# The sample's output projection in seven block products, with w_out's differences made beside w_in's pairs

## The chip, the cores and the metric

The kernel runs on one core of a Trainium2 chip. A core has TensorE for matmuls (PE in the profile; PEld is its weight load), VectorE (DVE), ScalarE (ACT), GpSimd (POOL) and SyncE (SP), whose queue issues nearly all DMAs. Each engine takes its own instructions in its own order and waits on semaphores for the others. Matmuls write to PSUM, of which the kernel uses eight banks of 128 x 512 fp32; SBUF holds everything else on the core. The metric is the device time of one execution in microseconds, the median over runs.

## The reference

One encoder layer on a prompt of 256 rows and a sample of 1024 rows, width 1024, with the same weights:

```
z = rmsnorm(x, g_mix) @ w_in                      # 1024 -> 5120: q, k, v of two branches, and gates
o_a = windowed attention with a sink (8 heads);  o_b = dilated attention (12 heads in 3 groups, merged)
merged = gates_a * (o_a @ w_a) + gates_b * (o_b @ w_b)
x = x + merged @ w_out                            # the output projection, 1024 x 1024
h = rmsnorm(x, g_mlp)
y = rmsnorm(x + square(relu(h @ w_up)) @ w_down, g_final)      # width 4096 inside
```

All of it is fp32. The kernel keeps the accuracy with matmuls on the type fp32r by splitting: a value becomes a high part (ACT copies it to the type fp32r) and a low part (DVE subtracts the high part), and a product is three matmuls: low by high, high by low, high by high.

## The kernel before, in words

The rows are ten tiles of 128: tiles 0 to 7 are the sample, 8 and 9 the prompt. The stages follow each other: values and normed x; w_in's columns in pairs (nine pairs alone, then seven beside the dilated attention); the windowed attention beside the last gates; the gate products; the output projection; the up projection; the down projection.

w_in's pairs, the up and the down projection already use the scheme of seven products (Strassen and Winograd): the sample's rows and the weight are cut into 2 x 2 blocks, A11 to A22 and B11 to B22, and instead of eight block products there are seven, of sums and differences: S1 = A21 + A22, S2 = S1 - A11, S3 = A11 - A21, S4 = A12 - S2 on the left, and T1 = B12 - B11, T2 = B22 - T1, T3 = B22 - B12, T4 = B21 - T2 on the right. The prompt's rows go through as plain products. `six` (line 342) issues the matmuls of one block product on one bank; `mm3` (line 188) the plain form.

*w_in's pairs.* `pair` (line 1039) issues the products of two columns of 128. Between them it calls `tick` (line 1115) 18 times a pair: it issues stores that are two ticks old, and later moves the dilated attention. `right_pair` (line 369) loads the next pair's weights on SP, makes the differences on POOL and the splits on ACT and DVE.

*Slots.* Nearly all SBUF is 33 slots of 4 KB a partition (`slot`), ten more for weights (`wslot`) and eight narrow ones (`qslot`). A tile gets a slot when one is free; the first instruction that writes it, often a DMA on SP, waits for the slot's last reader.

*Order.* Within `manual_schedule` each engine's instructions stand in the order in which the program writes them. That held for everything except the first half of the output projection, whose order a planner chose.

*The gate products* (loop at line 1527) are 48 products of 12 or 6 matmuls; each result is multiplied by its gate and added into `mT` on DVE. The list `side` beside them holds the splits that come next. w_out's blocks are loaded by `fetch` and split by `prepare` here and later.

*The output projection* (line 1646 on): for each half hh of the 1024 output columns and each of the ten tiles, 24 matmuls of 128 x 512 into one "mm" bank, then DVE adds the bank to the row tile `x2[t]`. Two tiles ahead, `split_m` splits `mT`. In the second half each tile is finished at once: ACT squares the row and takes the root (`ss`, `sd`), DVE scales it to `xn[t]`, SP stores the row to `scr_x`, and one tile later PE turns `xn` (`turned`, eight transposes, two banks) and ACT copies the turned tile out (`turn_sample`, `turn_prompt`). `more` and `sums` interleave w_up's first pair and the sums S1 to S3 of the turned rows. The prompt's tile 8 is turned in this loop, tile 9 in the up projection.

*The start of the up projection* (`up`, line 1947, with j = 0): the products A11, A12, S2, S3, S1, A22, then the next pair's A11 and A12, then S4 and the prompt. Between them `next(hooks)` runs one step of `entering` (line 2014): S3's split; tile 9 turned and S1's split; A22's split; S4's sums and split (`combine_last`); the prompt's split. `steps_of(b, 2)` runs what is left of the pair's own splits: none before, since the projection did them all.

## Time and profile before

| | |
|---|---|
| median of 3 runs | 1670.73 us (1670.70 to 1670.93) |
| the profiled execution's own time | 1671.05 us |
| its span, first to last instruction | 1669.3 us |
| PE busy | 1658.3 us, 9217 matmuls |
| DVE, ACT, POOL busy | 954.1, 715.1, 484.8 us |
| granted clock, mean | 0.999 |
| matmuls of the output projection | 480, first at 766.0 us |

Matmuls are pipelined: the duration of one overlaps the next, so PE shows as busy nearly all the time, and its pace is read from the distance between starts. In the chain of waits and in a timeline a row gives the start, the length, the engine and line, and in brackets the idle time before it with what ended it. In a table of stretches each engine's busy time stands in the order PE, PEld, DVE, ACT, POOL, then the granted clock, the DMA engines' share and GB/s.

### The profile page before, as it was taken

What the parts mean: (1) busy time and instruction counts of PE and PEld (TensorE: products, weight loads), DVE (VectorE), ACT (ScalarE), POOL (GpSimd) and SP (SyncE); (2) the same over time, 40 slices, a digit from 0 to 9 for tenths busy, and PEclk for the clock granted to TensorE, in tenths of its full rate; (3) what the DMA queues carried; (4) which work ended last, traced back from release to release, by engine and by line L of the source; (5) the groups of instructions that cost most, each with busy time, mean ns of one, the idle gap of its engine ahead of it and who ended that gap; (6) DMA issues with size and microseconds to landing.
All of it is one profiled execution on the core that took longest, in us unless ns stands there. A gap on an engine that the chain in (4) does not pass through costs nothing.

```text
span 1669.3 us, 24690 instructions
## 1 busy us (share of the span) xinstructions
PE 1658.3 (99%) x9217; PEld 1410.3 (84%) x9217; DVE 954.1 (57%) x1535; ACT 715.1 (43%) x1473; POOL 484.8 (29%) x362
## 2 busy tenths in 40 slices
PE   9999999999999999999999999999999999999998
PEld 7898888888888888788888888888888888888886
DVE  6732233455654565677378455455456775867665
ACT  6232323345654565654176333333334333333435
POOL 1212222121112353000100555455554250514240
PEclk9999999999999999999999999999999999999999
DMA  7416562666667795965111443343356934733333
GB/s 257 150 53 127 135 126 78 169 185 200 187 192 220 196 236 162 254 203 202 46 81 59 161 161 125 117 161 130 113 191 235 359 115 136 253 102 108 120 121 126
DMA packets 226993, 265.11 MB, mean 159 GB/s; under 512 B 29663, under 2 KB 156511, under 8 KB 226873
## 3 DMA queue, kind: packets, MB, share of 16 engines
q1 hardware_dynamic: 219816, 245.35, 46.5%
q0 software_dynamic: 6720, 17.65, 5.3%
q8 instruction: 73, 1.20, 0.3%
q10 hardware_dynamic: 336, 0.53, 0.1%
q14 instruction: 48, 0.39, 0.1%
HBM read 177.75 MB, written 90.96 MB: 161 GB/s over the span
## 4 chain that ended last, share of the span: by engine, by line
PE 95%; DVE 2%; ACT 1%; DMA 1%; issue 0%; SPq 0%; ACTq 0%
PE dn L346 22%; PE x L346 20%; PE mm L192 13%; PE z L346 10%; PE v L820 6%; PE y L346 5%; PE mm L346 5%; PE sc L346 3%; PE pv L346 3%; PE pv L1210 2%; PE pt L1194 2%; PE sc L554 1%; PE pv L601 1%; PE pt L587 1%; PE tr L337 1%; DMA sg<-scr_g 1%
## 5 line engine op out<-in xcount | busy, mean ns | idle before, releaser
L346 PE MATMUL dn<-dhi,ulo 128*128 128x512 f32 x448 | 174.3, 389 | 0.0
L346 PE MATMUL dn<-dlo,uhi 128*128 128x512 f32 x448 | 174.3, 389 | 0.0
L346 PE MATMUL dn<-dhi,uhi 128*128 128x512 f32 x448 | 174.3, 389 | 0.0
L346 PE MATMUL x<-chi,wlo 128*128 128x512 f32 x424 | 166.5, 393 | 0.0
L346 PE MATMUL x<-clo,whi 128*128 128x512 f32 x424 | 165.6, 390 | 0.0
L346 PE MATMUL x<-chi,whi 128*128 128x512 f32 x424 | 165.0, 389 | 0.0
L313 DVE TENSOR_TENSOR wlo<-ta,whi 128x1024 fp32r<-128x1024 f32 x30 | 55.7, 1855 | 173.4 <-ACT whi L311 173.4
L392 POOL TENSOR_TENSOR tb<-raw 128x512 f32<-128x512 f32 x25 | 32.7, 1307 | 410.6 <-PE mm L192 159.2
L313 DVE TENSOR_TENSOR wlo<-raw,whi 128x1024 fp32r<-128x1024 f32 x60 | 89.7, 1496 | 103.7 <-ACT whi L311 101.0
L346 PEld LDWEIGHTS dn<-dlo,uhi 128*128 128x128 f32 x448 | 84.1, 188 | 17.5
L346 PEld LDWEIGHTS dn<-dhi,uhi 128*128 128x128 f32 x448 | 84.1, 188 | 17.4
L346 PEld LDWEIGHTS dn<-dhi,ulo 128*128 128x128 f32 x448 | 84.1, 188 | 17.3
L346 PEld LDWEIGHTS x<-chi,whi 128*128 128x128 f32 x424 | 79.6, 188 | 16.9
L346 PEld LDWEIGHTS x<-chi,wlo 128*128 128x128 f32 x424 | 79.8, 188 | 15.2
L346 PEld LDWEIGHTS x<-clo,whi 128*128 128x128 f32 x424 | 79.8, 188 | 14.6
L1755 POOL TENSOR_TENSOR t<-raw,t 128x1024 f32<-128x1024 f32 x16 | 45.7, 2870 | 148.6 <-DMA raw<-in_w_down_dram 148.5
L186 DVE TENSOR_TENSOR ulo<-uraw,uhi 128x1024 fp32r<-128x1024 f32 x56 | 86.1, 1558 | 4.5 <-ACT uhi L185 4.5
L1906 DVE TENSOR_TENSOR v<-v,dn 128x512 f32<-128x512 f32 x90 | 59.7, 683 | 40.5 <-PE dn L346 38.5
L2006 POOL TENSOR_TENSOR u<-u,u 128x640 f32<-128x640 f32 x16 | 25.1, 1570 | 179.0 <-ACT u L1924 179.0
L186 DVE TENSOR_TENSOR dlo<-raw,dhi 128x1024 fp32r<-128x1024 f32 x32 | 50.5, 1601 | 45.2 <-ACT dhi L185 44.2
L346 PE MATMUL dn<-dhi,up 128*128 128x512 f32 x224 | 73.5, 389 | 0.0
L346 PE MATMUL z<-chi,wlo 128*128 128x512 f32 x184 | 71.6, 389 | 0.0
(319 smaller groups left out, 4605.3 us busy)
## 6 DMA issues: line engine op xcount, KB each, us to landing
scr_u<-u SPq DMA_DIRECT2D x112, 320.0 KB, 2.6
uraw<-scr_u SPq DMA_DIRECT2D x56, 512.0 KB, 4.4
raw<-in_w_down_dram SPq DMA_DIRECT2D x36, 512.0 KB, 7.0
raw<-in_w_up_dram SPq DMA_DIRECT2D x32, 512.0 KB, 5.5
raw<-in_w_in_dram SPq DMA_DIRECT2D x25, 512.0 KB, 5.4
sg<-scr_g SPq DMA_DIRECT2D x32, 256.0 KB, 5.9
uraw<-scr_u SPq DMA_DIRECT2D x28, 256.0 KB, 4.4
qk<-scr_kb SPq DMA_DIRECT2D x48, 128.0 KB, 2.8
```

The source lines that it names most:

```text
L186: nc.vector.tensor_tensor(lo, src, hi.bitcast(F32), op=ALU.subtract)
L192: nc.tensor.matmul(ps, a, b, start=i == 0, stop=i == len(seq) - 1)
L313: nc.vector.tensor_tensor(lo, src, hi.bitcast(F32), op=ALU.subtract)
L337: nc.tensor.transpose(ps[:, P * i : P * (i + 1)], xn[t][:, P * k : P * (k + 1)], ident)
L346: nc.tensor.matmul(ps, a, b, start=first and i == 0, stop=last and i == len(seq) - 1, skip_group_check=True)
L392: (nc.vector if vector else nc.gpsimd).tensor_tensor(o, x, y, op=ALU.subtract)
L820: nc.tensor.matmul(ps[:, :n], a, b, start=k == 0 and j == 0, stop=k == KC - 1 and j == 2)
L1194: nc.tensor.transpose(ps[:, P * k : P * k + P], s[:, h, P * b : P * b + P], ident)
L1210: nc.tensor.matmul(pv[HALVES[h], P * i : P * i + P], src, pt[:, at + 2 * b + h, :], start=b == 0, stop=b == W // P - 1, skip_group_check=True)
L1755: nc.gpsimd.tensor_tensor(o, a, b, op=ALU.subtract)
L1906: nc.vector.tensor_tensor(v, v, ps, op=ALU.add)
L2006: nc.gpsimd.tensor_tensor(u[S1], u21, u22, op=ALU.add)
```

## The change

Four parts.

1. *Differences ahead of time.* `differences` runs beside w_in's nine first pairs, one step a tick. In 16 rounds it loads a 128-column piece of w_out's four blocks into one slot (`wx`), makes T1 to T4 of it on DVE (in the order T1 and T3, T2, T4), splits them and stores high and low parts in DRAM (`scr_w`).
2. *Seven products.* Class `Out` writes the sample's projection as the products A12 by B21, S1 by T1, S4 by B22, A11 by B11, S2 by T2, S3 by T3, A22 by T4, each for four row tiles of 12 matmuls. A product's bank is added to one quarter of the rows (`TO`) and, where the scheme asks for it, stays open for the next product. T1 to T4 come from DRAM (`given`), the four blocks of w_out are loaded and split (`load`, `right`).
3. *36 steps in written order.* Each step is one group of 12 matmuls. The prompt's two tiles are cut by blocks: steps 4, 5, 18, 19 and 32 to 35. The list `side` gives each step's splits, sums, scalings and loads. `norm` (square, root, store) of tiles 0 to 3 is in steps 20 to 23, of tiles 4 to 7 in 28 to 31, of 8 and 9 in 33 and 35; `scale` follows in the next steps, and sample tiles are turned at the start of steps 23 to 26 and 31 to 34.
4. *The start of the up projection.* Both prompt tiles are scaled (behind S1's split) and turned (tile 8 behind `combine_last`, ahead of the product S1; tile 9 ahead of A22) there, and half of w_up's first pair's splits are left for it. S3's sums are made whole after the last turned tile.

```diff
         specs.append((w_b3[:, :, P * c : P * c + 4 * P], (P, 2, 4 * P), wslot))
     for c in range(0, KC, 2):
         specs.append((w_a3[:, :, P * c : P * c + 2 * P], (P, 4, 2 * P), wslot))
-    for h in range(2):
-        for i in range(4):
-            specs.append((w_out3[:, 2 * i : 2 * i + 2, 512 * h : 512 * h + 512], (P, 2, 512), wslot))
-    specs[n_out + 2] = specs[n_out + 2][:2] + (slot,)
     taken, raws = [0], []
...
+    scr_w = [dram.tile([P, 4, 4, 512], F32, name=f"scr_w{i}") for i in range(2)]
     scr_h = [dram.tile([P, 2, 2, 512], F32, name=f"scr_h{i}") for i in range(2)]
...
+        def differences():
+            blocks = w_out[0].rearrange("(a k p) (b c) -> p k a b c", a=2, p=P, b=2)
+            for i in range(16):
+                k, cols = i // 4, slice(P * (i % 4), P * (i % 4) + P)
+                x = slot("wx", (P, 8, P))
+                for a in range(2):
+                    nc.sync.dma_start(x[:, 2 * a : 2 * a + 2], blocks[:, k, a, :, cols])
+                for _ in range(3):
+                    yield
+                nc.vector.tensor_tensor(x[:, 4:6], x[:, 1:4:2], x[:, 0:2], op=ALU.subtract)
+                yield
+                nc.vector.tensor_tensor(x[:, 6], x[:, 3], x[:, 4], op=ALU.subtract)
+                nc.vector.tensor_tensor(x[:, 7], x[:, 2], x[:, 6], op=ALU.subtract)
+                yield
+                hi = stage("z", (P, 4, P), F32R, 2)
+                nc.scalar.activation(hi, x[:, 4:], AF.Copy)
+                yield
+                nc.vector.tensor_tensor(x[:, 4:].bitcast(F32R), x[:, 4:], hi.bitcast(F32), op=ALU.subtract)
+                yield
+                nc.sync.dma_start(scr_w[0][:, :, k, cols], hi.bitcast(F32))
+                nc.sync.dma_start(scr_w[1][:, :, k, cols], x[:, 4:])
+                yield
+                yield
+        apart = differences()
         def tick():
             ticks[0] += 1
             flush()
+            next(apart, None)
             n = ticks[0] - 18 * MIXED
             if n > 0 and n % 3 == 1:
                 next(att_b, None)
                 if first:
+                    run(apart)
                     att_b = attention_b(stage)
...
+        ORDER = (A12, S1, S4, A11, S2, S3, A22)
+        TO = (C11, C22, C12, C11, C12, C22, C21)
+        FIRST, LAST = (0, 1, 3), (0, 2, 6)
...
+        def load(self, name, k, h):
+            b = self.raw[name] = [self.make("oraw", (P, 2, 512)) for _ in range(2)]
+            for i in range(2):
+                j = 4 * k + 2 * i
+                nc.sync.dma_start(b[i], w_out3[:, j : j + 2, 512 * h : 512 * h + 512])
+        def right(self, name, i, make=wslot):
+            hi, lo = make("whi", (P, 2, 512), F32R), make("wlo", (P, 2, 512), F32R)
+            split(hi, lo, self.raw[name][i])
+            self.rights.setdefault(name, []).extend((hi[:, k, :], lo[:, k, :]) for k in range(2))
+        def given(self, name, n):
+            out = self.rights[name] = []
+            for i in range(2):
+                parts = [wslot("wt", (P, 2, 512), F32R) for _ in range(2)]
+                for x, src in zip(parts, scr_w):
+                    nc.sync.dma_start(x.bitcast(F32), src[:, n, 2 * i : 2 * i + 2, :])
+                out += [tuple(x[:, k, :] for x in parts) for k in range(2)]
...
+        def left(self, n, i):
+            hi, lo = slot("mhi", (P, 2, 512), F32R), slot("mlo", (P, 2, 512), F32R)
+            split(hi, lo, self.source(n, i))
+            self.lefts.setdefault(n, []).append((hi, lo))
+        def sum1(self, i):
+            self.s1.append(slot("s1m", (P, 2, 512)))
+            nc.vector.tensor_tensor(self.s1[i], mT.t[1, i], mT.t[1, 2 + i], op=ALU.add)
+        def sum2(self, i):
+            nc.vector.tensor_tensor(self.s1[i], self.s1[i], mT.t[0, i], op=ALU.subtract)
+        def sum3(self, i):
+            nc.vector.tensor_tensor(mT.t[1, i], mT.t[0, i], mT.t[1, i], op=ALU.subtract)
+        def sum4(self, i):
+            nc.vector.tensor_tensor(mT.t[0, 2 + i], mT.t[0, 2 + i], self.s1[i], op=ALU.subtract)
+        def split_prompt(self, k):
+            his, lo = [qslot("mph", (P, NP), F32R) for _ in range(4)], slot("mpl", (P, 4, NP), F32R)
+            src = mT.t[2, k]
...
+            self.pm[k] = [(his[c], lo[:, c, :]) for c in range(4)]
+        def add(self, t, h, ps):
+            v = x2[t][:, 512 * h : 512 * h + 512]
+            nc.vector.tensor_tensor(v, v, ps, op=ALU.add)
+        def product(self, n, t, name):
+            if n in self.FIRST:
+                tags = ("pt", "pt", "sc", "sc") if n == 1 else ("mm", "mm", "mm", "pv")
+                self.banks[t] = bank(tags[t], "wo")
+            lefts = [tuple(x[:, k % 2, P * t : P * t + P] for x in self.lefts[n][k // 2]) for k in range(4)]
+            six(self.banks[t], self.rights[name], lefts, n in self.FIRST, n in self.LAST)
+            c = self.TO[n]
+            return t + 4 * (c // 2), c % 2, self.banks[t]
+        def prompt(self, t, k, name, ps, first=True, last=True):
+            cols = slice(P * (t - 8), P * (t - 7))
+            six(ps, self.rights[name], [(hi[:, cols], lo[:, cols]) for hi, lo in self.pm[k]], first, last)
...
@@ -1529,15 +1629,24 @@
             load_gate(i + 8)
             for f, t in side_loads.get(i, ()):
                 f(t)
-            if i in (3, 24, 26, 31, 34, 38, 42):
+            if i in (3, 24, 26):
                 fetch()
-            if i > 41:
-                load_x2(i - 42)
+            if i == 28:
+                att_pool.close()
+                late = pre.enter_context(tc.tile_pool(name="late", bufs=1))
+                out.make = lambda name, shape=(P, D), dt=F32: late.tile(list(shape), dt, name=name, tag="l4", bufs=6)
+                out.load("b21", 1, 0)
+            if i in (40, 41, 42, 43):
+                load_x2(i - 40)
             open_gate(i + 2)
             for f, t in side.get(i, ()):
                 f(t)
-            if i in (38, 40, 42, 46):
-                prepare()
+            if i in (37, 39):
+                out.right("b21", (i - 37) // 2)
+            if i in (40, 41):
+                out.left(0, i - 40)
+            if i in (42, 44):
+                out.sum1((i - 42) // 2)
...
-            if i > len(jobs) - 6:
-                next(early_m, None)
-        run(split_m(1, 0, second_m))
-        last.close()
-    att_pool.close()
-    for t in range(len(x2), NT):
-        load_x2(t)
-        for q in (slice(0, 3 * P), slice(3 * P, 4 * P)):
+        for q in (slice(0, 2 * P), slice(2 * P, 3 * P), slice(3 * P, 4 * P)):
             for i in range(2):
                 nc.vector.tensor_tensor(s1[i][:, :, q], a21[i][:, :, q], a22[i][:, :, q], op=ALU.add)
-                yield
                 nc.vector.tensor_tensor(s2[i][:, :, q], s1[i][:, :, q], a11[i][:, :, q], op=ALU.subtract)
-                yield
-            for i in range(2):
-                nc.vector.tensor_tensor(a21[i][:, :, q], a11[i][:, :, q], a21[i][:, :, q], op=ALU.subtract)
-                yield
+            yield
+        for i in range(2):
+            nc.vector.tensor_tensor(a21[i], a11[i], a21[i], op=ALU.subtract)
...
+    def norm(t):
+        xn[t] = slot("xn", (P, D))
+        ss = small.tile([P, 1], F32, name="ss")
+        nc.scalar.activation(xn[t], x2[t], AF.Square, accum_out=ss)
+        sds[t] = small.tile([P, 1], F32, name="sd")
+        nc.scalar.activation(sds[t], ss, AF.Sqrt, bias=eps, scale=1.0 / D)
+        nc.sync.dma_start(scr_x[t], x2[t])
+    def scale(t):
+        rs = small.tile([P, 1], F32, name="rs")
+        nc.vector.reciprocal(rs, sds.pop(t))
+        nc.vector.scalar_tensor_tensor(xn[t], x2[t], rs, gm, op0=ALU.mult, op1=ALU.mult)
+    def first_left(k, i):
+        act[(A11, A12)[k]][i] = slot("chi", (P, 2, 512), F32R), slot("clo", (P, 2, 512), F32R)
+        split(*act[(A11, A12)[k]][i], raws_h[0, k][i])
...
+    def two():
+        steps_of(b0, 2)
+    gm = None
+    out.given("t1", 0)
+    for t in range(8, NT):
+        load_x2(t)
+    for t in range(4, 8):
+        load_x2(t)
+    out.load("b22", 1, 1)
+    S = lambda f, *a: (f, a)
+    keep = lambda name, shape, dt: out.make(name, shape, dt)
+    side = [[S(out.split_prompt, 1), S(out.left, 1, 0)], [S(out.left, 1, 1)], [S(out.sum2, 0)], [S(out.sum2, 1)],
+            [S(out.sum4, 0)], [S(out.sum4, 1)],
+            [S(out.left, 2, 0)], [S(out.left, 2, 1), S(out.right, "b22", 0, keep)], [S(out.right, "b22", 1, keep)],
+            [S(out.load, "b11", 0, 0), S(out.left, 3, 0)],
+            [S(out.right, "b11", 0)], [S(out.right, "b11", 1), S(out.left, 3, 1)],
+            [S(out.given, "t2", 2), S(out.sum3, 0)], [S(out.sum3, 1)],
+            [S(out.split_prompt, 0)], [S(out.left, 4, 0)], [S(out.left, 4, 1)], [S(load_g), S(out.left, 5, 0)],
+            [S(out.left, 5, 1)], [S(out.given, "t3", 1)],
+            [S(out.left, 6, 0)], [S(scale, 0)], [S(scale, 1)], [S(out.given, "t4", 3), S(out.load, "b12", 0, 1), S(scale, 2)],
+            [S(next, b0), S(scale, 3)], [S(next, b0), S(out.left, 6, 1)], [S(two)],
+            [S(first_left, 0, 0), S(first_left, 0, 1)],
+            [S(out.right, "b12", 0)], [S(scale, 4), S(first_left, 1, 0)], [S(scale, 5), S(out.right, "b12", 1)],
+            [S(scale, 6)], [S(scale, 7), S(first_left, 1, 1)], [S(next, sums)], [S(next, sums), S(two)], []]
+    plan = [(0, t) for t in range(4)] + [(8, 1, "b21"), (9, 1, "b21")]
+    plan += [(n, t) for n in (1, 2, 3) for t in range(4)] + [(8, 0, "b11"), (9, 0, "b11")]
+    plan += [(n, t) for n in (4, 5, 6) for t in range(4)]
+    names = ("b21", "t1", "b22", "b11", "t2", "t3", "t4")
+    for step in range(36):
+        turning = iter(())
+        if 23 <= step < 27:
+            turning = turn_sample(step - 23)
+        elif 31 <= step < 35:
+            turning = turn_sample(step - 27)
+        next(turning, None)
+        done = None
+        if step >= 32:
+            t = 8 + (step - 32) // 2
+            if step % 2 == 0:
+                ps = bank("sc", "wo")
+                out.prompt(t, 1, "b22", ps, last=False)
...
-            for t in range(NT):
-                m = parts.pop(t)
-                ps = bank("mm")
-                run(mm3(ps, [(m[k], (ws[k // 2][0][:, k % 2, :], ws[k // 2][1][:, k % 2, :]))
-                             for k in range(KC)]))
-                if hh == 0:
-                    nc.vector.tensor_tensor(x2[t][:, sl], x2[t][:, sl], ps, op=ALU.add)
-                    part(t + 2)
-                    if 2 <= t < 6:
...
-                turning = (turn_sample if t < 9 else turn_prompt)(t - 1) if t else iter(())
-                next(turning, None)
-                nc.vector.tensor_tensor(x2[t][:, sl], x2[t][:, sl], ps, op=ALU.add)
-                xn[t] = slot("xn", (P, D))
...
-                nc.vector.scalar_tensor_tensor(xn[t], x2[t], rs, gm, op0=ALU.mult, op1=ALU.mult)
-                nc.sync.dma_start(scr_x[t], x2[t])
-                next(turning, None)
...
+                out.prompt(t, 0, "b12", ps, first=False)
...
+        else:
+            n, t = plan[step]
+            done = out.product(n, t, names[n])
+        next(turning, None)
+        if done:
+            out.add(*done)
+        if 20 <= step < 24 or 28 <= step < 32:
+            norm(step - 20 if step < 24 else step - 24)
+        elif step in (33, 35):
+            norm(8 + (step - 33) // 2)
+        for f, a in side[step]:
+            f(*a)
+    run(sums)
+    run(halves(S2, combined[S2]))
+    last.close()
+    pre.close()
+    ctx.enter_context(tc.manual_schedule(engines=ALL))
...
             run(halves(S3, combined[S3]))
             yield
+            run(halves(S1, combined[S1]))
+            scale(8)
+            scale(9)
+            yield
+            run(halves(A22, combined[A22]))
+            yield
+            combine_last()
+            run(turn_prompt(8, ("pt", "sc")))
+            yield
             run(turn_prompt(9, ("pt", "sc")))
-            run(halves(S1, combined[S1]))
-            yield
-            run(halves(A22, combined[A22]))
-            yield
-            combine_last()
-            yield
             yield
             split_prompt()
             yield
```

93 lines of the change are left out of this document (31 added, 62 removed).

## The prediction

> **What bounds the kernel now.** I read the page first: its span, the busy times and the chain of work that ended last.
>
> ```profile
> span 1669.3 us, 24690 instructions
> ...
> PE 1658.3 (99%) x9217; PEld 1410.3 (84%) x9217; DVE 954.1 (57%) x1535; ACT 715.1 (43%) x1473; POOL 484.8 (29%) x362
> ...
> PE 95%; DVE 2%; ACT 1%; DMA 1%; issue 0%; SPq 0%; ACTq 0%
> ```
>
> TensorE sets the time: 95% of the chain is PE. So a matmul removed is worth its pitch, and another engine's work costs nothing until PE has to wait for it. The second view is the chain in order of time around the output projection, then one line's instructions.
>
> ```profile
> 832.32 5.46 PE mm L192 x24
> 838.66 5.46 PE mm L192 x24
> ...
> 892.52 2.72 PE z L346 x12
> ...
> 897.96 2.72 PE z L346 x12
> ```
>
> ```profile
> L192 PE MATMUL mm<-whi,mlo x160: 389/389/476, 766.0 to 881.3; 128*128 128x512 f32 x160
> ```
>
> The duration of one matmul (389 ns) overlaps its neighbour's. The pitch is what counts: 5.46/24 = 2.72/12 = 0.227 us. The eight transposes that turn a tile fill the gap 838.66 - 832.32 - 5.46 = 0.88 us. The projection is 3 x 160 = 480 matmuls from 766.0 on: 480 x 0.227 = 108.8, with nine turned tiles 7.9 more, 116.7. The next PE work begins at 881.96 (row below), 116.0 after the start, so PE never stops there. The waits of PE from 700 to 900 us confirm it:
>
> ```profile
> PE mm L192 <- DVE mT L1551: 1.1, 1, 1.1
> PE y L346 <- ACT praw L1577: 0.2, 1, 0.2
> ```
>
> The third view is busy time by stretch of 10 us.
>
> ```profile
> 760.00:770.00 10.00, 10.00 (x68) 9.27 (x67) 8.33 (x19) 4.18 (x13) 0.00 (x0) 1.00 1.02 405
> ...
> 800.00:810.00 10.00, 10.00 (x46) 8.28 (x45) 2.29 (x7) 0.00 (x0) 5.07 (x4) 1.00 0.00 1
> ...
> 880.00:890.00 10.00, 9.83 (x52) 8.02 (x51) 9.90 (x16) 6.30 (x11) 0.00 (x0) 1.00 0.56 154
> 890.00:900.00 10.00, 10.00 (x46) 8.28 (x45) 9.96 (x10) 7.28 (x10) 0.00 (x0) 1.00 0.02 5
> ```
>
> The columns are PE, PE's weight loads, DVE, ACT, POOL. In the middle of the projection DVE is idle three quarters of the time. Where the up projection starts (880 to 900) DVE is full (9.90 and 9.96 of 10) and PE only just does not wait. That is the place to watch.
>
> **What the change removes.** 36 steps of 12 matmuls are 432, so 48 matmuls go: 48 x 0.227 = **10.9 us**. Turned tiles are ten in both kernels. The new path from the first matmul to the end of step 35 is 36 x 2.72 + 8 x 0.88 = 105.0 us where nothing waits. All splits, additions and sums then have to fit into steps of 2.72 us (3.60 with a turned tile) instead of tiles of 5.46 (6.34).
>
> **What a step's chain costs.** The order is as written on each engine. In a step with `norm` and a split, DVE adds, ACT squares and takes the root, ACT copies the high part, DVE makes the low part, and only then may DVE add the next step. The durations (DVE and ACT timelines):
>
> ```profile
> 826.04 0.69 DVE L1682 TENSOR_TENSOR x<-x,mm 128x512 f32<-128x512 f32 x1 [4.75 <-PE mm L192]
> 832.30 0.68 DVE L1682 TENSOR_TENSOR x<-x,mm 128x512 f32<-128x512 f32 x1
> 832.90 1.22 DVE L313 TENSOR_TENSOR wlo<-raw,whi 128x1024 fp32r<-128x1024 f32 x1
> 834.52 0.16 DVE L1692 RECIPROCAL rs<-sd 128x1 f32<-128x1 f32 x1 [0.41 <-ACT sd L1687]
> 834.72 1.28 DVE L1693 SCALAR_TENSOR_TENSOR xn<-x,rs,gm 128x1024 f32<-128x1024 f32 x1
> 835.92 1.44 DVE L186 TENSOR_TENSOR mlo<-mT,mhi 128x256 fp32r<-128x256 f32 x4
> ```
>
> ```profile
> 827.93 1.28 ACT L1687 ACT_TABLE_LOAD   x1
> 829.23 0.29 ACT L1687 ACTIVATE sd<-ss,eps 128x1 f32<-128x1 f32 x1
> ...
> 830.66 1.05 ACT L311 ACTIVATE whi<-raw 128x1024 fp32r<-128x1024 f32 x1
> ...
> 834.20 0.29 ACT L1687 ACTIVATE sd<-ss,eps 128x1 f32<-128x1 f32 x1
> ```
>
> An addition takes 0.69 (0.60 to the next DVE instruction), a high part 1.05, a low part 1.22, `scale` 0.16 + 1.28 (1.40 in a row). From an addition's start to the root: 3.48 at the first tile, because of the table load, then 834.49 - 832.30 = 2.19. I let DVE start 0.2 after the step's last matmul is issued.
>
> *Tile 0* is turned at the start of step 23; its `scale` is in step 21, behind step 20's split of `left(6,0)`. From the end of step 20: 0.2 + 3.48 = 3.7 root, 4.7 high part, 5.9 low part, 6.4 after the addition of step 21, 7.9 `scale`. PE is there after two steps, 5.44: it waits **2.5**. The table load alone is 1.28 of it.
>
> *Tile 4* is turned in step 31; `scale(4)` stands in step 29, behind step 28's `norm` and `right("b12", 0)`. Same chain with the short root: 0.2 + 2.19 + 1.05 + 1.22 + 0.6 + 1.45 = 6.7 against 5.44: 1.3. To this comes w_up. How long loads of 512 KB take, shortest, median and longest, by w_in's in the pairs:
>
> ```profile
> DMA to landing us min/median/max: 4.0/5.4/8.5
> ```
>
> w_up's first raw is the seventh 512 KB load that SP issues after step 23 (four of `t4`, two of `b12`): 7 x 0.524 MB at the 405 GB/s of the row for 760 us is 9.1, SP starts about 0.9 after the step because it stands behind the store of tile 3, and the landing adds about 2.7 (the shortest 4.0 less 1.3 of transfer). So it lands 12.7 after step 23. ACT wants it after three steps of 3.60, at 10.8. ACT's high parts of step 26 and 27 then end at 13.8, 14.7, 15.7 and DVE's last low part at 17.9; step 28's addition was due at 16.4. 1.5 later: tile 4 waits **2.7**, bounds 1.3 (load early) and 5 (load 2.5 later).
>
> *Tiles 5 and 6* follow steps that again hold addition, root, high and low part in series, 0.69 + 1.48 + 1.05 + 1.22 = 4.4 (1.48: the 2.19 less the addition and its handing over), against 3.60: **0.75** each. Together 6.7 in the middle.
>
> A rule of the Trainium skill bears here ("SBUF — State Buffer", section "SBUF: two separate sides"): a DVE instruction with two inputs in SBUF and a GpSimd instruction that reads SBUF exclude each other for a whole instruction. The trace agrees:
>
> ```profile
> 952.36 1.75 POOL L392 TENSOR_TENSOR ta<-raw,tb 128x512 f32<-128x512 f32 x1
> ...
> 952.88 2.31 DVE L313 TENSOR_TENSOR wlo<-raw,whi 128x1024 fp32r<-128x1024 f32 x1
> ```
>
> That low part takes 2.31 instead of 1.22, behind a difference that GpSimd had begun. GpSimd's four differences of w_up fall into steps 27 and 28 by the sum above; by the rule tile 4 would wait one to two such delays, 1.1 to 2.2, longer, and the end would be 1678.3 to 1679.4. I leave it out of the sum: there, where each step's chain waits for ACT, DVE has gaps that can take it.
>
> **The end, where DVE is full.** Step 35's addition is the last thing of the projection; all that follows stands behind it on DVE. The rows of before:
>
> ```profile
> 881.96 1.03 PE L337 MATMUL tr<-ident,xn 128*128 128x128 f32 x8
> ...
> 883.76 0.41 DVE L1604 TENSOR_TENSOR s<-hraw 128x256 f32<-128x256 f32 x1
> 884.21 0.43 DVE L1606 TENSOR_TENSOR s<-s,hraw 128x256 f32<-128x256 f32 x1
> ...
> 887.46 2.35 DVE L313 TENSOR_TENSOR clo<-s,chi 128x1024 fp32r<-128x1024 f32 x2
> ...
> 889.73 2.36 DVE L313 TENSOR_TENSOR clo<-hraw,chi 128x1024 fp32r<-128x1024 f32 x2
> ...
> 890.49 1.09 ACT L1577 ACTIVATE praw<-tr 128x512 f32<-128x512 f32 x2
> ...
> 892.00 0.68 DVE L1927 TENSOR_TENSOR u<-y,c 128x512 f32<-128x512 f32 x1
> ...
> 893.33 2.36 DVE L313 TENSOR_TENSOR clo<-s,chi 128x1024 fp32r<-128x1024 f32 x2
> ...
> 899.00 2.35 DVE L1617 TENSOR_TENSOR hraw<-hraw,s 128x1024 f32<-128x1024 f32 x2
> ```
>
> ```profile
> 900.32 2.20 ACT L185 ACTIVATE chi<-hraw 128x1024 fp32r<-128x1024 f32 x2 [3.03 <-DVE hraw L1617]
> ```
>
> A pair of low parts or sums is 889.73 - 887.46 = 2.27, one is 1.14; relu and square 893.33 - 892.00 = 1.33; four sums of a 256 quarter 1.6. From the end of step 35 on DVE: start 0.2, addition 0.6, last quarter 1.6, S3 sums 2.27, S2 2.27, `tb` 1.14, S3 2.27, relu 1.33, `raw[1]` 1.14, S1 2.27, `scale(8)` 1.4: **16.5**. PE reaches tile 8's transposes after A11, A12, S2, S3 = 10.9: it waits about 5.6 (a part of it already at S2 and S3). New in this list against before are `tb`, `raw[1]`, one more `scale`, and S3's sums whole instead of their last quarter (2.27 for 0.8): 5.2 us on an engine without room.
>
> Next: `scale(9)` 17.9, A22 20.2, the next pair's first low part 21.3, the S4 sums 23.7. ACT has S4's high parts ahead of tile 8's two copies: 24.7, then 25.8. PE turned tile 8 until 17.5 and did S1 until 20.2. Tile 9's second half needs an "sc" bank; one is held by `z`, the other by tile 8 until that copy. So PE waits until 25.8, and A22 starts at **26.3** (half a turn later). Before it started at 897.96 - 881.96 = 16.0 after the projection, with the same transposes and groups between. Cost 10.3. Upper bound: one port delay and one late load more, 13. Lower bound: without the bank wait, A22's low parts are still at 20.2, so A22 starts at about 20: 4.
>
> **Beside w_in's pairs.** 16 rounds of two loads, three small differences, a split and two stores. DVE's work is at most 3 x 0.42 for the differences (256 elements a row or fewer) and 0.69 for the low part, 2.0 a round, 31 us in nine pairs where DVE is under a third busy:
>
> ```profile
> 100.00:200.00 100.00, 100.00 (x539) 89.09 (x538) 29.21 (x27) 27.70 (x40) 21.64 (x21) 1.00 0.56 119
> ```
>
> w_in's own loads land after 5.4 (row above). A wait for a 256 KB load stands on DVE just behind the addition of `y` or `x`, and the next of these that PE needs comes over 2.7 later, so a load that lands at 5.4 is hidden; the long store row of the query pairs on SP may delay one or two. I take 0.5, bounds 0 and 4 (three rounds at 8.5 less 2.7 would be more, but not all meet a matmul). **Steps 0 to 19** need 1.9 to 3.3 a step on DVE (an addition and one to three low parts or sums), 2.0 on average, under 2.72. Their loads: `t1`, six x tiles and b22 are 12 x 0.524 MB, 15.5 at 405 GB/s, from the last gate products on; x is wanted from step 4 (13.6), b22 in step 7 (21.8). b11 waits for b22's splits of step 8, lands about when ACT wants it in step 10, and has until step 14. Nothing; if that cover is gone, the load's lateness counts.
>
> **Sum.** From the first matmul to A22: 105.0 + 6.7 + 26.3 = 138.0; before 897.96 - 766.0 = 132.0. +6.0, with the pairs +6.5. The profiled run took 1671.05 (span 1669.3); its median is 1670.73, 0.3 less. 1671.05 + 6.5 - 0.3 = **1677.2**. The 10.9 saved are more than given back as waits.
>
> **Rivals.**
>
> *The order does not bind, and it gets faster.* If `scale` and the copies of tiles 8 and 9 ran when ready (both roots are ready 3 us after step 35), PE would wait for none of the turned tiles in the middle, and at the end A22 would be late only by DVE's 5.2 more work. Then 105.0 + 21 = 126 against 132: 1670.7 - 6 + 0.5 = 1665. The point: `scale(8)` ends less than 10.9 after step 35. For it speaks that ACT has room there; against it that ACT's `chi` at 900.32 sat 3.03 idle for DVE with later work ready behind.
>
> *The clock falls in the long waits.* The granted clock in the last stretches:
>
> ```profile
> 1660.00:1665.00 5.00, 2.56 (x12) 1.78 (x10) 2.70 (x7) 3.08 (x8) 0.00 (x0) 1.00 0.54 210
> 1665.00:1670.00 5.00, 0.00 (x0) 0.00 (x0) 0.37 (x1) 0.40 (x1) 0.00 (x0) 0.53 0.27 105
> ```
>
> It falls to 0.53 a few us after the last matmul. PE would idle 4.5 and 5.6 us at tiles 8 and 9; if the 12 matmuls after each ran at 0.53, that is 2 x (2.72/0.53 - 2.72) = 4.8: 1682. The Trainium skill ("TensorE: Matmul & The Clock Gate", Part 1) says that the clock halves after an idle window of about 3.4 us; no wait before is that long, so this trace shows only the end.
>
> *The scratch path blocks the pairs.* SP waits for the slot of the differences until both stores land, and w_in's loads queue behind. If each of the nine pairs lost 0.7: 1683. Against: a round has nine of a pair's 18 ticks, over 10 us (seven groups of 2.72 and two of the prompt a pair), for two landings of 5.4.
>
> *The waits come to two thirds of the sum* (w_up early, low parts not needed at a group's first matmul): 11.3 instead of 17.0, 1670.7 - 10.9 + 11.3 + 0.5 = 1671.6.
>
> **Numbers.** Forecast 58%, free order 13%, clock 11%, pairs 6%, two thirds 12%. A change under 0.2% (3.3 us) cannot be told here. Slower: forecast, clock, pairs, less the forecast's own lower edge, 0.71; same 0.16; faster 0.13. The forecast's own range is 1672 to 1682 (middle 5 to 9, end 7 to 13); the range for all is 1668 to 1684.
>
> **What would show it.** Right: PE waits for `xn` at the transposes of tiles 0, 4, 5, 6 and 8 (2.5, 2.7, 0.75, 0.75, about 4.5) and for the prompt copy at tile 9 (about 5.5); 9169 PE matmuls; DVE full for 25 us behind step 35. Wrong: PE without waits from 766 to 910, or waits in the pairs between 119 and 345, or a granted clock under 1 near 890.

## The result, and the profile after

The changed kernel takes **1718.02 us** (median of 6 runs, 1714.69 to 1719.62) against 1670.83 beside it (1670.56 to 1671.13): 1.0279 times, 95% interval 1.0266 to 1.0293. That is 47.2 us slower. The forecast was 1677.2, its range ended at 1684: the sign was right, the size far off. The profiled execution took 1716.08 (span 1714.3), 45.0 more than the one of before; the places below are read from it.

The page of the changed kernel, the same lines as before:

```profile
span 1714.3 us, 24750 instructions
...
PE 1663.6 (97%) x9169; PEld 1410.0 (82%) x9169; DVE 992.7 (58%) x1565; ACT 715.8 (42%) x1431; POOL 496.0 (29%) x362
...
PE 84%; DMA 7%; DVE 4%; ACT 2%; issue 1%; SPq 1%; POOL 0%; DVEq 0%; ACTq 0%; POOLq 0%
```

The 48 matmuls are gone (9217 to 9169), yet PE is busy 5 us longer, and DMA's share of the chain has grown from 1% to 7%. Stretches of the span show where (PE, weight loads, DVE, ACT, POOL, then PE's granted clock):

```profile
100.00:200.00 100.00, 88.86 (x463) 78.52 (x462) 32.83 (x43) 26.74 (x40) 19.31 (x18) 0.95 0.63 145
...
860.00:865.00 5.00, 4.29 (x16) 3.67 (x17) 2.61 (x4) 3.27 (x10) 0.00 (x0) 0.66 0.51 210
...
935.00:940.00 5.00, 0.33 (x3) 0.09 (x1) 5.00 (x5) 2.97 (x4) 0.00 (x0) 0.97 0.00 0
```

Before, PE was busy for 100 of 100 in the first row, at clock 1.00. What PE waits for, first from 95 to 400, then from 700 to 960:

```profile
PE x L341 <- ACT c L1079: 10.8, 4, 3.5
PE x L341 <- DVE long L965: 10.2, 1, 10.2
```

```profile
PE tr L332 <- DVE xn L1739: 5.1, 2, 2.7
PE tr L332 <- ACT praw L1677: 4.8, 1, 4.8
PE tr L332 <- DVE rs L1738: 2.5, 1, 2.5
```

So there are two losses. In **w_in's pairs** PE waits 21.0 us. The first product of the projection starts at 795.57 (timeline), not at 766.0: 29.6 later, and the 8.6 that no wait explains are slow matmuls behind the waits. From **the projection's first product to A22's** it takes 941.28 - 795.57 = 145.7 instead of 132.0: 13.7 more. Together 43.3 of the 45.0; A22's own group, at a slow clock, is 1.0 more (3.68 for 2.72), and 0.7 has no place yet.

The pairs, by the chain of waits:

```profile
129.08 19.82 DMA scr_w<-wx
...
148.99 0.59 SPq L1118
...
149.63 2.64 DMA wx<-in_w_out_dram
...
152.46 0.43 DVE wx L1121
152.88 0.99 DVE long L965
...
153.91 4.94 PE x L341 x12
158.86 2.75 PE y L341 x12
```

A store of the differences (256 KB) takes 19.82. SP waits for it, because the next round's load goes into the same slot. Then DVE waits for that load (L1121), and behind it on DVE stands `long` (L965), the addition that PE waits for. PE then needs 4.94 for 12 matmuls, 2.2 more than its usual 2.72.

The up projection's start, by the same view:

```profile
909.19 5.47 PE wo L341 x24
...
917.98 2.27 DVE hraw L1708 x2
920.25 4.54 DVE clo L308 x4
...
935.72 2.28 DVE hraw L1715 x2
...
938.09 1.06 ACT chi L185
939.14 0.98 ACT praw L1677 x2
...
940.17 1.11 PE tr L332 x4
941.28 3.68 PE z L341 x12
```

Step 35 ends at 914.66, A22 starts at 941.28, 26.6 later. This is the prediction's chain: DVE's list, S4's sums and high part ahead of the prompt's copy, then tile 9's second half.

### The profile page after: what moved, and what is told of

It reads as the page before. It is cut to its first block, busy times and chain, and to the rows that moved or that the text cites. A ratio compares the mean times of both kernels' runs of the same rounds, so it can differ in the third digit from the quotient of the medians.

```text
span 1714.3 us, 24750 instructions
## 1 busy us (share of the span) xinstructions
PE 1663.6 (97%) x9169; PEld 1410.0 (82%) x9169; DVE 992.7 (58%) x1565; ACT 715.8 (42%) x1431; POOL 496.0 (29%) x362
## 4 chain that ended last, share of the span: by engine, by line
PE 84%; DMA 7%; DVE 4%; ACT 2%; issue 1%; SPq 1%; POOL 0%; DVEq 0%; ACTq 0%; POOLq 0%
PE dn L341 22%; PE x L341 16%; PE z L341 8%; PE mm L192 8%; PE v L816 6%; PE wo L341 4%; DMA scr_w<-wx 4%; PE y L341 4%; PE mm L341 3%; PE sc L341 3%; PE pv L341 3%; PE pt L1219 1%; PE pv L1235 1%; PE sc L550 1%; PE pv L597 1%
## 5 line engine op out<-in xcount | busy, mean ns | idle before, releaser
L387 POOL TENSOR_TENSOR tb<-raw 128x512 f32<-128x512 f32 x25 | 37.4, 1496 | 502.5 <-DMA raw<-in_w_up_dram 314.1
L341 PE MATMUL z<-clo,whi 128*128 128x512 f32 x184 | 72.2, 392 | 0.0
```

Source lines behind the costliest of these rows:

```text
L341: nc.tensor.matmul(ps, a, b, start=first and i == 0, stop=last and i == len(seq) - 1, skip_group_check=True)
L387: (nc.vector if vector else nc.gpsimd).tensor_tensor(o, x, y, op=ALU.subtract)
```

## Experiments

Each time is a median. The kernel before, run beside each of them, took 1670.7 to 1672.2.

**No rounds.** The rounds of differences are left out; the projection loads parts of h21 in their place.

```diff
-        apart = differences()
+        apart = iter(())
-                for x, src in zip(parts, scr_w):
-                    nc.sync.dma_start(x.bitcast(F32), src[:, n, 2 * i : 2 * i + 2, :])
+                for x, src in zip(parts, scr_h):
+                    nc.sync.dma_start(x.bitcast(F32), src[:, i])
```

> The differences are left out: no rounds beside w_in's pairs; the projection loads parts of h21 in the place of the four differences, so its output is not the reference's. Its work is the same. Theory 1 (the rounds cost what is lost between 119 and 360): TensorE does not wait in the pairs, 29.6 us come back, about 1688.5. Rival (the pairs lose by something else, such as another placing of code or data): 1710 to 1718. If 1688 comes, the rest, 17 to 18 us over before, is the projection and the start of the up projection alone.

Measured: 1687.98 (1.0104 [1.0089, 1.0119] times before). PE waits for nothing between 95 and 400; the first product of the projection starts at 765.43, and A22 911.74 - 765.43 = 146.3 later, as in the changed kernel (145.7). The rounds cost all of the 30 us; what is left, 17, belongs to the projection and the up projection's start.

**Own raw blocks.** The next load no longer waits for the stores of the round before.

```diff
-                x = slot("wx", (P, 8, P))
+                r = stage("z", (P, 4, P), F32, 2)
...
+                x = slot("wx", (P, 8, P))
...
-                hi = stage("z", (P, 4, P), F32R, 2)
+                hi = x[:, :4].bitcast(F32R)
```

> The raw blocks of a round go into the two z tiles, the high parts over the slot's own first half: the next round's loads on SP no longer wait for the stores of the round before; DVE's first difference does, five ticks later. Theory 1a (one slot: SP's load waits for slow stores, and everything behind it is late): at least two thirds of the 29.6 come back, 1690 to 1699. Rival 1b (the loads of 512-byte pieces are themselves late beside GpSimd's broadcasts, whatever they wait for): 1708 to 1718.

Measured: 1715.11. My first theory fell: PE still waits 21.0. The chain of waits of this run:

```profile
122.79 20.45 DMA z<-in_w_out_dram
...
143.36 0.44 DVE wx L1122
...
145.01 0.59 ACT c L1079
145.59 0.04 issue
145.64 5.49 PE x L341 x12
```

Now the load itself, 128 KB, takes 20.45. The tile `wide` of this run, from 90 to 365:

```profile
L295 POOL DMA_DIRECT2D wide<-scr_l x6: 700/704/907, 120.4 to 259.3; - x6
...
DMA to landing us min/median/max: 10.4/10.7/22.3
```

GpSimd issues its first broadcast (2 MB, the longest) at 120.4; with 22.3 it ends at 142.7, the load at 143.24.

**No stores.** The rounds compute, but store nothing.

```diff
-                nc.sync.dma_start(scr_w[0][:, :, k, cols], hi.bitcast(F32))
-                nc.sync.dma_start(scr_w[1][:, :, k, cols], x[:, 4:])
```

> The rounds make the differences and their parts but do not store them; the projection loads parts of h21 in their place, so its output is not the reference's. Theory 1a: the slot is free as soon as the low part is made, SP never waits for a store, and nearly all comes back: 1689 to 1693. Rival 1b: the loads still wait behind the broadcasts: 1705 to 1715.

Measured: 1697.41 (1690.62 to 1700.67), between the two theories: 20.6 of the 30 come back. Loads land after 4.0 in the median, 16.1 at most. Stores and loads are both late.

**Broadcasts elsewhere.** GpSimd's six broadcasts go into the stage of the values, whose rows are then stored from SP's queue.

```diff
+            if t == 5:
+                run(line(0))
...
+            if t in (5, 6, 7, 8, 9):
+                run(line(t - 4))
...
-                        hooks = line(j) if j < len(LINES) else iter(())
+                        hooks = iter(())
...
-            nc.gpsimd.dma_start(scr_v[rows, 512 * v : 512 * v + NV[v]], vo)
+            nc.sync.dma_start(scr_v[rows, 512 * v : 512 * v + NV[v]], vo)
```

> GpSimd's six broadcasts to wide stand in the stage of the values (one after the store of the lines, five in its second half), not beside the pairs; that stage's value rows are stored from SP's queue. The rounds of differences are unchanged. Theory 1c (a load or store of 512-byte pieces lands only with the end of a broadcast that runs beside it: 128 KB in 20.5 us for 122.8 to 143.2 in the run with the raw blocks apart): every landing in the pairs falls to some 3 us, TensorE waits nowhere in them, 1686 to 1692. Rival 1d (the rounds' place in the order on SP, DVE and ACT, without the broadcasts): above 1705.

Measured: 1712.07. The total says no, the trace says yes. The tile `scr_w` between 95 and 365, and PE's waits from 0 to 400:

```profile
DMA to landing us min/median/max: 2.6/2.8/5.4
```

```profile
PE v L816 <- ACT vo L824: 10.0, 1, 10.0
PE tr L332 <- DVE xn L761: 7.9, 5, 5.5
PE x L341 <- ACT c L1083: 3.2, 1, 3.2
```

Beside no broadcast a store lands in 2.8, at most 5.4, and the pairs lose 3.2. But the value rows, which now run beside the broadcasts, are late in their turn, and PE waits there. The loss follows the broadcasts. The expectation had 1686 to 1692 for the whole kernel and missed it for those rows.

**Stores in pieces of 2 KB**, a quarter of the packets.

```diff
-    scr_w = [dram.tile([P, 4, 4, 512], F32, name=f"scr_w{i}") for i in range(2)]
+    scr_w = [dram.tile([P, 4, 4, 4, P], F32, name=f"scr_w{i}") for i in range(2)]
-                nc.sync.dma_start(scr_w[0][:, :, k, cols], hi.bitcast(F32))
+                nc.sync.dma_start(scr_w[0][:, k, i % 4], hi.bitcast(F32))
...
```

> The differences are stored in pieces of 2 KB, not 512 bytes (16384 packets fewer beside the pairs); they are read back in pieces of 512 bytes in the projection. Broadcasts and loads stay where they are. If a store beside a broadcast is late by its number of packets, its 19.8 us fall to about 5, and what the run without stores gained (20.6 us) comes back for the most part: 1698 to 1706. If it is late because the broadcast goes first, whatever the number: 1714 to 1720.

Measured: 1716.2, with 36848 packets from 95 to 365 instead of 49129 (12281 fewer; the 16384 above was a miscount). The same tile:

```profile
DMA to landing us min/median/max: 2.0/2.4/19.2
```

Alone it is faster (2.4 for 2.8), beside a broadcast as late as ever. The number of pieces is not it.

**Broadcasts in 28 pieces**, one head at a time, one in five ticks.

```diff
-        nc.gpsimd.dma_start(wide, scr_l[h0 : h0 + n, first : first + length].unsqueeze(0).to_broadcast([P, n, length]))
+        for h in range(n):
+            row = scr_l[h0 + h : h0 + h + 1, first : first + length]
+            nc.gpsimd.dma_start(wide[:, h : h + 1], row.unsqueeze(0).to_broadcast([P, 1, length]))
+            yield
...
+            if ticks[0] % 5 == 2:
+                next(heads, None)
...
```

> The six broadcasts are cut head by head into 28 of 128 to 256 KB, one in five ticks (7 us); nothing else is changed. Theory 1e (a load or store beside a broadcast lands with the end of that broadcast, whatever its number of pieces, so it is the length of one broadcast that counts): no landing is later than some 6 us, the waits of 21.0 us and the slow clock behind them go for the most part: 1688 to 1698. Rival 1f (the time of all the broadcasts together counts, or the rounds are too dense for the queue): above 1708.

Measured: 1693.44. `scr_w` lands after 3.9, at most 7.0, and all that PE waits for from 95 to 400 is

```profile
PE x L343 <- ACT c L1081: 3.0, 1, 3.0
```

The same bytes in shorter broadcasts give back 24.6 of 30. That is the time that theory 1e foretold, but its reason, the length of one broadcast, is not shown. GpSimd issues the pieces in bursts of three or four, and a store that is issued inside a burst still lands behind the last piece. The tile `wide` of this run from 161 to 165, then `scr_w` from 165 to 167:

```profile
L298 POOL DMA_DIRECT2D wide<-scr_l x4: 523/523/526, 161.6 to 163.1; - x4
...
DMA to landing us min/median/max: 4.7/6.3/7.1
```

```profile
L1133 SPq DMA_DIRECT2D scr_w<-z x1: 577/577/577, 165.6 to 165.6; - x1
...
DMA to landing us min/median/max: 7.0/7.0/7.0
```

The last of the four pieces lands at 163.1 + 7.1 = 170.2, the store, which has 640 KB of SP's own ahead of it, at 165.6 + 7.0 = 172.6. In the run with the broadcasts elsewhere, five whole ones were issued within 2.5 us, and a value store behind them (and behind 2 MB of SP's own stores) took 25.66. Its tile `wide` from 86 to 90, and its chain of waits:

```profile
L295 POOL DMA_DIRECT2D wide<-scr_l x5: 726/951/1187, 86.4 to 88.9; - x5
...
DMA to landing us min/median/max: 12.5/24.3/28.4
```

```profile
90.33 25.66 DMA scr_v<-vo
```

So what these runs show is that the time counts for which broadcasts are in flight together: 28 us (two that overlap, 120.3 to 148.3) and then 10.2 to 11.8 in the changed kernel, 6.9 to 9.7 in pieces. Whether the length of one piece counts besides, no run separates. The Trainium skill ("DMA: Bandwidth & Descriptors", "Queues, rings and completion order") says that an engine alternates between queues and drains a whole packet of several descriptors from one before it turns to the next. In the changed kernel from 178 to 182, with three transfers of SP's issued, all 70 packets are of GpSimd's queue, which fits; in the run with the broadcasts elsewhere, from 92 to 112, packets of both queues run side by side (613 and 633), and the store is late all the same. How the packets are grouped no run here shows.

**Loaded one round ahead**, broadcasts whole.

```diff
+            raw = []
+            for i in range(17):
...
+                if i < 16:
+                    raw.append(stage("z", (P, 4, P), F32, 2))
...
+                r, k, cols = raw[i - 1], (i - 1) // 4, slice(P * ((i - 1) % 4), P * ((i - 1) % 4) + P)
```

> The broadcasts stay whole and where they are, the projection is as in the changed kernel. Only the rounds differ: raw blocks in the z tiles, loaded nine ticks (12.5 us) before they are used. If the lack of slack makes the loss, a load that is 10 us late no longer holds DVE, and 15 to 25 of the 29.6 us come back: 1693 to 1703. If the length of a broadcast makes it whatever the slack (the stores hold the slot, w_in's own loads stand behind the rounds' DMAs on SP): 1710 to 1718.

Measured: 1703.44, 14.6 back, just past the first theory's range. In the rest of the pairs, beside the broadcasts of 10 to 12 us, nine ticks more of slack leave PE 3.5 of wait, where the run with own raw blocks had 8.1. The other 12.7 is one wait, for a load that lands after 20.7 beside the broadcast of 2 MB. That load is the first round's, and this edit does not bring it forward: the first two rounds are loaded together, and the first is used three ticks later. So slack beside the longest broadcast was not tried here. Both factors make the loss.

**w_up first.** One entry moves ahead on SP.

```diff
-             [S(out.given, "t4", 3), S(out.load, "b12", 0, 1), S(scale, 2)],
-            [S(next, b0), S(scale, 3)], ...
+             [S(next, b0), S(out.given, "t4", 3), S(out.load, "b12", 0, 1), S(scale, 2)],
+            [S(scale, 3)], ...
```

> Nothing but the order on SP: w_up's two raw loads stand ahead of t4's four and b12's two in step 23, not behind them. Theory 2 (w_up's raw, which landed at 881.7, 15.7 us after step 23, holds ACT, then DVE, then the additions of steps 27 to 31): they land about 9 us earlier, tile 4 waits for its short chain only, 3 to 6.5 us less: 1711.5 to 1715. Rival (the chain addition, root, split in series is the reason, or t4 and b12 are late in their turn): 1717 to 1720.

Measured: 1709.46, 8.6 less. In its profile the projection up to A22 takes 931.86 - 791.67 = 140.2, 5.5 less than 145.7, which is in the range of 3 to 6.5. The other 3, by which the time lies below the forecast, would be the pairs: the edit does not touch them, and their end is 3.9 earlier in this execution. w_up's lateness was the larger part of tile 4's wait.

**Tile 0**, on top of w_up first.

```diff
+    nc.scalar.activation(small.tile([P, 1], F32, name="sd"), eps, AF.Sqrt)
-            [S(out.left, 5, 1)], [S(out.given, "t3", 1)],
-            [S(out.left, 6, 0)], [S(scale, 0)], ...
+            [S(out.left, 5, 1)], [S(out.given, "t3", 1), S(out.left, 6, 0)],
+            [], [S(scale, 0)], ...
```

> As the run with w_up first, and the root's table is loaded before the projection by one small root, and left(6,0) is split in step 19 instead of 20. Theory 4 (tile 0 waits for 1.28 of table load and for the split that stands between root and scaling on DVE): tile 0 does not wait, 2.4 and the slow clock of 1.9 after it come back: 1704.5 to 1707 against 1709.5. Rival (the addition, square and root in series alone are longer than two steps): 1708 to 1710.

Measured: 1706.8. Tile 0 waits no more, and the projection up to A22 takes 930.99 - 794.59 = 136.4, 3.8 less. Table load and split together were the cause.

**The end.** Tile 8 is turned after S1, tile 9 after A22; S2's parts stand before S3's sums, `scale(9)` behind A22's parts.

```diff
-    run(sums)
+    next(sums)
     run(halves(S2, combined[S2]))
+    run(sums)
...
             combine_last()
+            yield
             run(turn_prompt(8, ("pt", "sc")))
             yield
             run(turn_prompt(9, ("pt", "sc")))
-            yield
             split_prompt()
```

> Behind step 35: S2's parts before S3's sums, tile 8 turned after S1 and tile 9 after A22, scale(9) behind A22's parts. Theory 3 (A22 starts 26.5 after step 35 because DVE is full and because tile 9's transposes wait for tile 8's copies behind S4's sums): tr no longer waits (2.5 + 4.8 and half a group's slow clock after each), A22's start is left to DVE, 18.5 to 21 after step 35; 1709 to 1713. Rival (DVE's total alone decides): A22 moves by scale(9)'s 1.4 and no more, 1716 to 1718.

Measured: 1715.63 (1711.74 to 1720.27), between theory and rival, 2.4 less and uncertain. A22 starts at 929.99 by the timeline, step 35 ended at 911.34: 18.7 instead of 26.6. But tile 9, now behind A22, still waits 4.3 for the prompt's copy behind S4's sums: more than half of the gain is given back one product later.

**All orders, no rounds.** The three edits above, and S4's split behind tile 9's copies.

```diff
     def combine_last():
...
+    def last_parts():
+        a12 = combined[S4]
...
             run(turn_prompt(9, ("pt", "sc")))
+            last_parts()
             split_prompt()
```

> No rounds (the projection loads parts of h21 in the place of the differences, so its output is not the reference's), and all orders put right: w_up first, root's table early, left(6,0) in step 19, S2's parts before S3's sums, scale(9) behind A22's parts, tile 8 turned after S1 and tile 9 after A22, S4's split behind the copies of tile 9. By the parts measured (1688.0 without rounds, less 8.5, less 4.3 at tile 0, less 5 to 9 at the end): 1665 to 1671. If the projection itself were bound by DVE's total, whatever the order: 1674 or more.

Measured: 1670.33 against 1671.49 (0.9998 [0.9989, 1.0008]). No wait of PE in the projection is over 1.2, and A22 starts 895.03 - 766.56 = 128.5 after the first product, 3.3 less than before by the same view (897.80 - 765.98). The gain is given back behind A22: against the kernel before, A22 is 2.8 early, the next product 1.8 (tile 9's turn, 0.9, now stands between), the next pair's product into `z` 0.8 (PE waits 0.6 there for a copy of ACT's), and the span is 0.7 shorter. Not all of that has a cause yet.

**All orders and short broadcasts**, with the raw blocks in the z tiles; the next run adds loads one round ahead and lets GpSimd make S3's and S4's sums.

```diff
-            nc.vector.tensor_tensor(a21[i], a11[i], a21[i], op=ALU.subtract)
+            nc.gpsimd.tensor_tensor(a21[i], a11[i], a21[i], op=ALU.subtract)
-            nc.vector.tensor_tensor(a12[i], a12[i], s2[i], op=ALU.subtract)
+            nc.gpsimd.tensor_tensor(a12[i], a12[i], s2[i], op=ALU.subtract)
```

> All together: the broadcasts in 28 pieces, the raw blocks of the rounds in the z tiles, and the orders of the run before. It computes all of the reference. If the pieces leave 0 to 10 us in the pairs: 1666 to 1680. By rival 1f: 1690 or more.

> The run before with two more edits: each round's blocks are loaded one round (nine ticks) earlier, and the sums of S3 and of S4 behind step 35 (two of 2.3 us on DVE) are made by GpSimd. It computes all of the reference. If a late load on SP's queue was what was left in the pairs (3.5 of wait, 2.7 of slow clock behind it), 4 to 6 of the 6.0 us come back; if DVE's list sets A22's start, 2 to 4.5 come back there: 1667 to 1671 against 1676.9. Rival: GpSimd's sums are late for S3 and S4 themselves (some 5 us a pair of sums against 2.3), and the end gains nothing: 1671 to 1674.

Measured: 1676.88 without, 1675.63 with the diff (1.0030 [1.0018, 1.0042]); the first is in its range, the second above both of its ranges. In the second the pairs are free of waits (0.4), but A22 comes 23.9 after step 35. DVE's and GpSimd's timelines there:

```profile
876.25 2.61 DVE L1716 TENSOR_TENSOR s<-hraw 128x256 f32<-128x256 f32 x1
...
882.40 6.70 DVE L310 TENSOR_TENSOR clo<-s,chi 128x1024 fp32r<-128x1024 f32 x2
889.02 2.35 DVE L310 TENSOR_TENSOR clo<-hraw,chi 128x1024 fp32r<-128x1024 f32 x2
```

```profile
876.02 2.56 POOL L1720 TENSOR_TENSOR hraw<-hraw 128x1024 f32<-128x1024 f32 x1 [29.64 <-DVE s L1716]
...
882.16 5.85 POOL L1727 TENSOR_TENSOR hraw<-hraw,s 128x1024 f32<-128x1024 f32 x2
```

A sum of 0.42 takes 2.61 beside GpSimd's 2.56, a pair of low parts 6.70 instead of 2.35 beside its 5.85. That is the rule of the Trainium skill which the prediction weighed ("SBUF — State Buffer", "SBUF: two separate sides"), and this run agrees.

**Those sums back on DVE**, and then w_up's last parts up to three steps earlier.

```diff
-            [S(scale, 6)], [S(scale, 7), S(first_left, 1, 1)], [S(next, sums)], [S(next, sums), S(two)], []]
+            [S(scale, 6), S(two)], [S(scale, 7), S(first_left, 1, 1)], [S(two), S(next, sums)], [S(next, sums), S(two)], []]
```

> As the run with GpSimd's sums, with those sums back on DVE. If DVE and GpSimd shut each other out (there a sum of 0.42 took 2.61 beside GpSimd's 2.56, and a pair of low parts 6.70 beside 5.85), A22 starts 18.9 after step 35 instead of 23.8: 1669 to 1672. Rival (the low parts were late for another reason): 1674 to 1677.

> As the run before it, and w_up's parts of ta, tb and raw[1] are made in steps 31, 33 and 34 instead of 34 and behind 35, so that three low parts of 1.2 us leave DVE's list behind step 35 or stand earlier. DVE has 3.4 of 10 us free in steps 31 to 33: A22 starts 2 to 3.5 earlier, 1667 to 1669.5. Rival (they only push the additions and sums of steps 33 to 35 back): 1670 to 1673.

Measured: 1672.09 against 1672.01 (1.0001 [0.9992, 1.0010]) without the diff, 1673.16 (1.0011 [1.0002, 1.0020]) with it. The first, which computes all of the reference, is the best of these versions and no faster than the kernel before. Its first product starts at 766.72, 0.7 later than before, so short broadcasts and a round of slack together cure the pairs; and A22 comes 18.7 after step 35, not 23.9, so it was the sums on GpSimd that made DVE late. In the second the rival's reason held (the time is 0.2 past its range): a moved low part holds step 35's addition on DVE, ACT's square of tile 9 waits 3.6 for it, S2's high part stands behind that, and PE waits 3.9. No version here beats the kernel before.

## Why the prediction was wrong, step by step

**The matmuls.** Right. The first 23 steps take 62.6 (795.57 to 858.2), 2.72 each, and steps 0 to 19 cost nothing.

**The pairs: the step that failed.** The prediction put them at "0.5, bounds 0 and 4", from "w_in's own loads land after 5.4". They cost 29.6. Three things were wrong. First, the price of a landing was taken from transfers that meet a broadcast only at its tail. The kernel before, on GpSimd and on SP:

```profile
161.39 0.70 POOL L300 DMA_DIRECT2D wide<-scr_l  x1
186.23 0.70 POOL L300 DMA_DIRECT2D wide<-scr_l  x1
```

```profile
169.45 5.18 SPq L377 DMA_DIRECT2D raw<-in_w_in_dram  x2
...
194.29 5.18 SPq L377 DMA_DIRECT2D raw<-in_w_in_dram  x2
```

A broadcast stands on GpSimd behind the differences of the blocks last loaded, and w_in's next loads come 8 us after it, near its end (it lands after 10.2 in the median). So 5.4, and even the 8.5 of the worst, said nothing on a load in its middle. The rounds, which run all the time, meet it everywhere: 19.8 and 20.5. The row that should have set the upper bound was the broadcast's own, in the kernel before:

```profile
wide<-scr_l POOLq DMA_DIRECT2D x1, 2048.0 KB, 21.6
```

Even that is not the whole: the first two broadcasts overlap, and are in flight for 28 us together. Second, the wait was held to be hidden because the next addition that PE needs comes over 2.7 us later; a wait of 10 or 20 stands in the middle of DVE's and ACT's queues, and the instructions that free PE's banks stand behind it (`long`, `c`). Third, PE's clock: 8.6 of the 29.6 are slow matmuls. The rival "the scratch path blocks the pairs" named a part of it (SP held by the slot's stores), with 0.7 a pair for what measured 3.3 a pair; but freeing SP from those stores alone gave next to nothing back (1715.11).

**The middle.** The sum held 6.7; the profile gives 914.66 - 795.57 = 119.1 from the first product to the end of step 35, 14.1 more than 105.0. Tile 0 waited 2.4 (2.5 predicted), for the reason given (shown by the tile 0 run). Its slow matmuls, 1.9, were not in the sum. Tile 4 was late by 6.8 for 2.7: PE idled 1.3 and 2.7, and between the two it did A11's product (2.7), of which more below. The chain of waits has two reasons:

```profile
870.89 10.77 DMA raw<-in_w_up_dram
...
886.17 2.31 DVE clo L186
```

w_up's raw landed at 881.66, 15.7 after step 23's end (865.99 on the timeline), not 12.7. That is 3.0 later, past the 2.5 of the upper bound; why is not shown. And a low part took 2.31 instead of 1.22 beside GpSimd's differences of w_up: the delay of 1.1 that the prediction left out, because DVE "has gaps that can take it", stood in tile 4's own chain. 2.7 + 3.0 + 1.1 = 6.8. The run with w_up first moves both, and PE waits 0.6 at tile 4. Tile 5 lost 0.4 and tile 6 nothing (0.75 each predicted; 4.4 less 3.60 would be 0.8). The last 2.6 of the 14.1 are slow matmuls behind tile 4 and small pieces.

**The end.** 26.3 predicted, 26.6 measured, with the waits named: 2.5 at tile 8, after 3.6 ahead of it at S2, and 4.8 at tile 9 (about 4.5 and 5.5). One thing was different: in the trace A11's product is not behind step 35 but ahead of step 31. The program writes it behind step 35; what moved it is not shown. It filled 2.7 of tile 4's wait, and the end, which DVE sets, did not get shorter for it.

**The clock rival** came true beside the forecast, not in its place: 0.66 in the row for 860, and 8.6 lost in the pairs alone, where it had put 4.8 at tiles 8 and 9. What a wait costs behind it varies. In the run with own raw blocks, a wait of 2.2 at 253.2 was followed by a clock of 0.66 up to 258 and 1.7 lost, one of 12.9 by 2.8 lost; in the run on the end, a wait of 3.1 at 279.5 was followed by a clock of 1.00 and no loss. The Trainium skill ("TensorE: Matmul & The Clock Gate", Part 1) speaks of an idle window of about 3.4 us; here 2.2 us of idle time could be enough.

**The sum.** Predicted +6.5. Measured in the profile +45.0: pairs 29.6, middle 7.4 more than put, the end 0.3 more, 1.7 behind it, and the 6.0 of the projection that were forecast. The sign did not hang on the pairs: without the rounds the kernel is still 17 slower, by waits at the tiles that the prediction named.

## What to carry to other kernels

Before transfers are put beside other work, look at what shares the queues with them at every moment at which they will run, and bound their landing by the time for which the long transfers there are in flight together, not by the median of a neighbour that was issued at a better moment. A load that is late costs what stands behind its waiter on the same engine, so a side job in written order needs a whole round of slack, and long broadcasts are better cut and spread out. A saving on the engine that sets the time is worth something only if the others' lists fit into the shorter stretch: here 10.9 us of matmuls were saved, the best order brought A22 forward by 3.3, and the kernel ended even, not faster.

## What was not expected of the hardware

A 128 KB load or a 256 KB store from SP takes up to 20.5 and 19.8 us beside a 2 MB broadcast of GpSimd's, 2.8 otherwise, and a store up to 25.7 with five broadcasts in flight; pieces of 2 KB in place of 512 bytes change nothing (19.2); the broadcasts in short pieces, spread out, do (7.0). PE's clock can fall after 2.2 us of idle time; twelve matmuls then take up to 5.5 instead of 2.72. A DVE sum of 0.42 took 2.61 beside a sum of GpSimd's.
